# Gaps in the SBUF pools, so that the operands of the long products begin at multiples of 128 bytes

## The chip, the cores and the metric

The kernel runs on one core of a Trainium2 chip. The core has a matrix engine (TensorE; PE in the rows, and PEld for its weight loads), a vector engine (VectorE, DVE), a scalar engine (ScalarE, ACT), GpSimd (POOL), SyncE (SP), which issues most transfers, and 16 DMA engines between HBM and the on-chip memories. SBUF holds operands in 128 partitions; a tile lies at the same byte address in each. PSUM takes the products. The metric is the time of one execution on the device, in microseconds.

## The reference

Two transformer blocks on 256 tokens of 2048 features, all in float32.

```python
# first block
h = h + mixer_sublayer(rms_norm(h, norm_mix[l]), w_in[l], ..., w_out[l])
h = h + peer_sublayer(rms_norm(h, norm_ffn[l]), peer_w_query[l], peer_sub_keys[l], peer_u[l], peer_v[l])
# peer_sublayer, of each block of 128 tokens
q = (hb @ w_query).reshape(PEER_BLOCK, PEER_HEADS, 2, D_KEY // 2)
...
a = jax.nn.gelu(jnp.einsum('thkd,td->thk', u_sel, hb), approximate=False)
return jnp.einsum('thk,thkd->td', (g * a).astype(hb.dtype), v_sel)
```

The mixer runs two kinds of attention over 16 meta tokens and the 256 tokens. The product-key experts choose 16 of 16384 experts per head and token. The second block has a modulation vector, attention beside a diagonal state space, two gated branches, and a feed-forward of 5632 hidden features with a causal convolution. Nearly all the arithmetic is in products of a weight [features in, features out] with the activations [features in, 256 tokens].

## The kernel before

**Products.** Activations lie with features on partitions, so a product takes 128 x 128 of a weight as the stationary operand and 128 features of all 256 tokens as the moving one (272 columns in the mixer, with the meta tokens). To keep float32's precision in the fast mode (float32r), each operand is split into a high and a low part, and `mm3` issues three products: high by high (L175), high by low (L176), low by high (L177). Each of the three loads its own weights; PE's records show a weight load (PEld) beside every product.

```python
mm(out, a[0], b[0], start=start, stop=False, **kw)
mm(out, a[0], b[1], start=False, stop=False, **kw)
mm(out, a[1], b[0], start=False, stop=stop, **kw)
```

**Stages**, in the order of time:
- the mixer (to some 500 us): its norm makes hh and hl with 272 columns, so 1088 bytes per row; heads go into tiles hd of the same size. The products of w_out read hd;
- the experts: queries, then scores of all experts against hh, hl of the next norm (1024 bytes per row), while routing runs; from about 950 to 2100 us the loop over expert rows does, per half step, 24 products with rows of v (stationary wp or, for odd rows, vp; moving ahi, alo) and 24 products of scores (stationary wp, moving hh, hl); a stretch of the former alone follows;
- attention and state space (2290 to 2750 us), with hh, hl of another norm and the pool's tiles b2 (named b in the trace); then the branches and the output product, whose moving operand is b2;
- the feed-forward (from about 3010 us): up products with hh, hl, down products with act, in four turns.

**Tiles.** A pool lays its tiles out in the order in which their names are first asked for, a ring of `bufs` copies for each, each address rounded to 32 bytes. The pool `glob` lives throughout and holds raw (a ring of 5 loads), constants, the residual xT, hh, hl, wp (a ring of 8 split weights) and the norm's scratch. Other pools are opened per stage behind it and hold hd, ahi, alo, vp, first, b2 and act.

```python
hi, lo = (self.sb(self.glob, "wp", [128, n, m], F32R, bufs=NWP) for _ in range(2))
...
hi, lo = (sb(spare["v"], "vp", [128, 1024], F32R, bufs=2) for _ in range(2))
...
hi, lo = (sb(spare["v"], nm, [128, T], F32R, bufs=10) for nm in ("ahi", "alo"))
...
A[j + f] = a = sb(pool, "act", [128, 2, T], F32R, bufs=26)
```

**Order.** The program's order is written out by hand: `Pipe` issues the loads and splits of a job between the products of the job one or two places before, and side work (attention heads, routing, state space, `ssm_parameters`) advances by a step behind each job. Weights come by SyncE's queue into raw, are split by ScalarE (L143) and VectorE (L144), and are multiplied. `ssm_parameters` (L1683) loads three small tables at the end of the experts' loop: raw takes two of them, the tiles ldt and sel2 of the pool `experts` stand beside it.

Of the kernel before, what the change touches and what calls it, by code (L numbers as in the profile page):

```python
# [8 lines left out]
F32 = mybir.dt.float32  # L9
# [15 lines left out]
EPS = 1e-6  # L25
# [11 lines left out]
class Pipe:  # L37
    """Issues jobs in order. A job is its preparation and its matmuls, each a function that may be a generator of steps;
    the preparation is issued between the steps of the matmuls of the job `depth` places before.
    Side work (generators) advances by one step behind each job, and behind those steps of it that `mid` names;  # L40
    so does `slow`, which nothing here completes."""
# [8 lines left out]
    @staticmethod  # L50
    def steps(f, *args):
        """f as a generator that returns f's result."""
        r = f(*args)
        if hasattr(r, "send"):
            r = yield from r
        return r
# [58 lines left out]
class Core:  # L115
# [13 lines left out]

    def ps(self, tag):  # L130
        return self.psum.tile([128, 512], F32, name=f"ps_{tag}", tag=f"ps_{tag}", bufs={"g": 2, "t": 2, "v": 4}[tag])

    def copy(self, out, in_):
        """A copy, on the scalar and the vector engine in turn."""
        self.flip ^= 1
        if self.flip:
            self.nc.scalar.copy(out, in_)
        else:
            self.nc.vector.tensor_copy(out, in_)

# [8 lines left out]
    def parts(self, kt, m):  # L149
        """The two parts of kt * 128 rows of m: tiles of at most 1024 elements per partition. Returns the tiles  # L150
        [(first k, n, hi, lo)] and the function of k that gives its parts."""
        per = 1024 // m
        tiles = []
# [6 lines left out]
    def split_w(self, loaded, kt, off, m):  # L160
        """The parts of a loaded weight's columns off .. off + m."""
# [10 lines left out]
    def mm3(self, out, a, b, start, stop, **kw):  # L172
        """out += a.T @ b for operands in two parts each (the product of the low parts, under 2^-24, is left)."""
        mm = self.nc.tensor.matmul
        mm(out, a[0], b[0], start=start, stop=False, **kw)  # L175
        mm(out, a[0], b[1], start=False, stop=False, **kw)  # L176
        mm(out, a[1], b[0], start=False, stop=stop, **kw)  # L177

    def load_w(self, w, r0, kt, c0, width, pieces=1):
        """[kt * 128, width] of a weight, in tiles of at most 2048 elements per partition: [(first kt, n, tile)]."""  # L180
# [16 lines left out]
    def gemm_jobs(self, w, r0, kt, c0, ncols, xs, n, post, group=256):  # L197
        """out[f, :n] = w[r0:r0 + kt * 128, c0 + f].T @ x, in feature tiles of 128; post(f tile, psum) takes each.
        xs(k) gives the parts of x's k-th 128 rows."""
# [23 lines left out]
    def lead(self, w, r0, c0, xs, n, post, before):  # L223
        """The first four feature tiles of a gemm of 16 k tiles whose x is made meanwhile: by before(c) for k = 4 c .. 4 c + 3,
        in two steps.
        A generator: its first step takes only the pools that live throughout, and the last job before it is issued there."""
# [63 lines left out]
    def columns(self, pool, name, vecs, stage, queue=None):  # L290
        """Vectors of DRAM, each a multiple of 128 long, as columns [128, n], and the generator that fills them:
        a tile of each 128 rows is turned on the PE."""
# [3 lines left out]
        at = 0  # L296
# [24 lines left out]
    def rstd(self, out, ss, n):  # L321
        """out = 1 / sqrt(ss / n + EPS)"""
# [5 lines left out]
    def head_sum(self, acc, h, sq, n):  # L328
        """Adds the sums of sq's columns as the rows h and 32 + h of acc."""
        self.nc.tensor.matmul(acc[:40, :n], self.sel[:, 7 - h:47 - h], sq, start=h == 0, stop=h == 7)  # L330

    def head_parts(self, out, src):
        """The parts of rows that are the same on h and 32 + h."""
# [3 lines left out]
    def head_row(self, h, n=128):  # L337
        """What a product with head_parts' rows takes to give row h on n partitions."""
        return self.both[:, h:h + 1].to_broadcast([40, n])

# [1 line left out]
    def sq_add(self, k, t):  # L342
        """Adds the squares of the residual's k-th tile; they are issued at the next call."""
# [24 lines left out]
    def norm(self, gains, shifts=None, table=None):  # L368
        """The parts of the normalised residual, x * rstd * gain (+ shift): a function of k, and one that makes
        the parts of k = 4 c .. 4 c + 3 in two steps, to be called for c = 0, 1, 2, 3."""  # L370
# [59 lines left out]
    def stagger(self, gens, every):  # L430
        """Side work: starts a generator every so many steps; a step of each live one per step, the oldest first."""
# [14 lines left out]
    def interleave(self, gens, width):  # L446
        """Side work: runs the generators, `width` of them at a time, a step of each per step."""
# [13 lines left out]
    def mixer(self, pool, upto):  # L461
# [46 lines left out]
        def gains():  # L508
            """What is needed later only."""
# [13 lines left out]
        # the rows, turned to [feature, position], 16 meta and 256 tokens: the residual, and its parts times the gain  # L523
        self.xT = [sb(self.glob, "xT", [128, T], bufs=KT) for _ in range(KT)]
        hh = sb(self.glob, "hh", [128, KT, N], F32R)
# [37 lines left out]
        def scales():  # L563
            """1 / rms of each position, along the free axis; the products take it behind."""
# [6 lines left out]
        def scaled(out, p, o, factor=None):  # L571
            """The product, scaled."""
# [7 lines left out]
        xs_tok = lambda k: (hh[:, k, NM:], hl[:, k, NM:])  # L580
        hd = lambda dt=F32: sb(pool, "hd", [128, N], dt, bufs=40)
# [10 lines left out]
        def values(key):  # L592
            """Values to [position, head dim], the positions in tiles of 128, 128 and 16."""
# [17 lines left out]
        # the heads' outputs times their gains, in parts, and the sums of the outputs' squares  # L611
# [18 lines left out]
        def scale_of(key):  # L630
            """1 / rms of the heads' outputs, on every partition."""
# [52 lines left out]
        # forget gates: log f = min(z, 0) - log(1 + exp(-|z|)), summed along the positions  # L684
# [18 lines left out]
        # forgetting attention  # L703
# [167 lines left out]
    def slowly(self, chunks, every):  # L871
        """Side work: a step of the modulation's first chunks every so many steps."""
# [5 lines left out]
    def modulate(self, chunks):  # L878
        """Completes the first chunks of the modulation."""
# [4 lines left out]
    def peer_head(self):  # L884
        """The norm and the first queries."""
# [17 lines left out]
    def peer(self, ctx, pool, upto):  # L903
# [16 lines left out]
        def start_u(i):  # L920
            """Expert rows i * 128 .. to [feature, expert], in parts: the step that turns the g-th four feature tiles,
            and the function of k that gives the parts."""
# [17 lines left out]
        def spill():  # L940
            """The parts of x to DRAM, [q, c, b, a, token] of feature 512 q + 128 a + 32 b + c."""
# [6 lines left out]
        def reorder():  # L948
            """The parts of x from DRAM: partition 32 q + c of tile 4 b + a."""
# [11 lines left out]
        def blocks(i):  # L961
            """As start_u, but turned on the vector engine in blocks of 32 x 32: partition 32 q + c of the k-th tile is
            feature 512 q + 32 k + c. Returns the step that turns a half and the one that parts it."""
# [17 lines left out]
        def scores(i, g, at):  # L981
            """A quarter of the scores."""
# [36 lines left out]
        def weights(b, chunks=slice(0, 16)):  # L1019
            """The weights of WI expert rows, [second key, chunk, first key, token]."""  # L1020
# [6 lines left out]
        def start():  # L1027
# [3 lines left out]
            def first(c, wc):  # L1031
                """The first weights, of the last chunks from where they are made."""
# [9 lines left out]
        def coef(i):  # L1042
# [5 lines left out]
            if i < 2:  # L1048
                hi, lo = (sb(wp, "first", [128, T], F32R, bufs=4) for _ in range(2))
            else:  # L1050
# [5 lines left out]
        def ahead(n):  # L1056
            """The coefficients for the n-th half step."""
# [10 lines left out]
        with self.tc.tile_pool(name="experts", bufs=1) as ep:  # L1068
            banks = {}
            spare["v"] = ep  # L1070

            def v_main(*ns):
                """The n-th half steps, of one half. Its first four tiles gather the sums of all experts, the others those of a block.
                Returns what adds the complete ones to the residual."""
# [34 lines left out]
            def half_step(n, block=None, half=0, ticks=0):  # L1109
                """The n-th half step, with the operands of the next, the coefficients of the second next and half of a block."""  # L1110
# [54 lines left out]
    def route(self, rp, wd, start_u, scores, spill, blocks, start, v_split, ahead):  # L1165
        """Weights of the chosen experts, [16 tokens' chunk, second key, first key, token], to DRAM; scores meanwhile."""
# [11 lines left out]
        def score():  # L1178
            """The scores of the next 128 experts as a job."""
# [21 lines left out]
        with self.tc.tile_pool(name="pick", bufs=1) as pool:  # L1201
# [3 lines left out]
            def turn_keys(g, bank):  # L1205
                """A quarter of the keys, turned; returns what moves them out."""
# [19 lines left out]
            def pick(vals, idx, src, width):  # L1226
                """The 16 largest of src's rows with their places, the earlier of equals first."""
# [193 lines left out]
    def reduce_angle(self, pool, a, shape, tag):  # L1421
        """a - 2 pi * round(a / (2 pi)), in place; 2 pi in three parts, of which the first two times a count are exact."""
# [11 lines left out]
    def sin_cos(self, sin, cos, a, tmp):  # L1434
        """Of angles in [-pi, pi]: the cosine is the sine of pi / 2 - |a|."""
# [5 lines left out]
    def mixing_head(self):  # L1441
        """The norm and the first inputs of the state space."""
# [7 lines left out]
    def mixing(self, pool):  # L1450
# [8 lines left out]
        # rotary tables  # L1459
# [21 lines left out]
        # projections  # L1481
# [9 lines left out]
        ssq = sb(pool, "ssq2", [40, 2, T], F32R)  # L1491

# [123 lines left out]
        # branches: gate = (1 + tanh) / 2, the half in the merged parts  # L1616
# [463 lines left out]
```

## Time and profile before

| | us |
|---|---|
| three runs | 3784.16, 3787.84, 3791.34 |
| median | 3787.84 |
| span of the profiled execution, first to last instruction | 3782.9 |
| TensorE busy / weight loads busy | 3702.9 / 3612.2 |
| VectorE / ScalarE / GpSimd busy | 2834.4 / 1820.2 / 479.0 |

The page gives the profiled execution's span alone; what lies around it is the difference to the runs, about 5 us. Busy time of PE is the union of records that overlap: a product's record lasts about 0.28 us, and the next begins some 0.11 to 0.13 us after it did. So a busy share near 100% doesn't tell how fast the products follow each other. That is read from counts in a window or from the starts in the timeline. A window counts every record that touches it.

### The profile page before, as it was taken

How to read it: one execution, taken by the hardware profiler on the slowest of the kernel's cores; microseconds unless marked ns; L12 is line 12 of the kernel's file. 1: busy time of each engine (PE TensorE's matmuls, PEld its weight loads, DVE VectorE, ACT ScalarE, POOL GpSimd, SP SyncE). 2: the span in 40 equal slices, each digit the busy share in tenths (PEclk: the TensorE clock that was granted, in tenths of full speed). 3: DMA queues.
4: the chain of work that ended last, by engine and by line, in shares of the span. 5: the costliest groups of instructions: out<-in, count | busy, mean ns of one | idle time of the engine just before them, and what ended most of it. 6: DMA issues, size and time to landing. Idle time of an engine off the chain costs nothing.

```text
span 3782.9 us, 72640 instructions
## 1 busy us (share of the span) xinstructions
PE 3702.9 (98%) x30186; PEld 3612.2 (95%) x30186; DVE 2834.4 (75%) x4414; ACT 1820.2 (48%) x2740; POOL 479.0 (13%) x496
## 2 busy tenths in 40 slices
PE   9999999999999999999999999899999999999998
PEld 8989899999999999999999999888889999999998
DVE  5555678977788888888888779999887675656565
ACT  4443443369444444444444456665544454444443
POOL 0000012100000000000000015666420100000000
PEclk9999999999999999999999999999999999999999
DMA  6546555445988888888888766555477665555563
GB/s 204 168 137 197 178 169 170 155 168 208 275 239 241 244 243 241 242 244 244 241 242 245 250 208 200 168 169 168 154 228 231 196 223 182 194 168 193 179 199 124
DMA packets 491481, 768.99 MB, mean 203 GB/s; under 512 B 21050, under 2 KB 332501, under 8 KB 485248
## 3 DMA queue, kind: packets, MB, share of 16 engines
q1 hardware_dynamic: 476160, 712.11, 61.2%
q0 software_dynamic: 14960, 52.23, 4.9%
q8 instruction: 237, 3.88, 0.4%
q14 instruction: 92, 0.75, 0.1%
q10 hardware_dynamic: 32, 0.01, 0.0%
HBM read 734.92 MB, written 27.26 MB: 201 GB/s over the span
## 4 chain that ended last, share of the span: by engine, by line
PE 83%; DVE 7%; ACT 5%; issue 2%; DMA 2%; POOL 1%; DVEq 0%; POOLq 0%; ACTq 0%
PE ps_g L175 19%; PE ps_g L177 19%; PE ps_g L176 19%; PE ps_v L175 4%; PE ps_v L176 4%; PE ps_v L177 4%; PE ps_t L175 3%; PE ps_t L176 3%; PE ps_t L177 3%; DVE wp L144 3%; ACT wp L143 1%; PE ps_t L934 1%; ACT raw L1366 1%; DMA raw<-in_peer_u_dram 1%; ACT hot_i L1381 1%
## 5 line engine op out<-in xcount | busy, mean ns | idle before, releaser
L175 PE MATMUL ps_g<-hh,wp 128*128 128x256 f32 (+1 forms) x5648 | 1629.0, 288 | 0.3 <-ACT wp L143 0.3
L177 PE MATMUL ps_g<-hh,wp 128*128 128x256 f32 (+1 forms) x5648 | 1606.9, 285 | 10.5 <-DVE wp L144 10.4
L176 PE MATMUL ps_g<-hl,wp 128*128 128x256 f32 (+1 forms) x5648 | 1604.6, 284 | 2.8 <-DVE hl L1614 2.8
L144 DVE TENSOR_TENSOR wp<-raw,wp 128x1024 fp32r<-128x1024 f32 (+2 forms) x877 | 1054.8, 1223 | 70.3 <-ACT wp L143 69.7
L175 PEld LDWEIGHTS ps_g<-hh,wp 128*128 128x128 f32 x5648 | 1079.8, 191 | 24.5 <-issue 15.6
L177 PEld LDWEIGHTS ps_g<-hh,wp 128*128 128x128 f32 x5648 | 1080.0, 191 | 14.3 <-DVE wp L144 13.5
L176 PEld LDWEIGHTS ps_g<-hl,wp 128*128 128x128 f32 x5648 | 1080.2, 191 | 3.7 <-DVE hl L1614 3.1
L143 ACT ACTIVATE wp<-raw 128x1024 fp32r<-128x1024 f32 (+2 forms) x877 | 869.4, 1014 | 379.0 <-PE ps_g L176 203.8
L862 DVE SCALAR_TENSOR_TENSOR macc<-raw,cs,macc 128x512 f32<-128x512 f32 x360 | 283.3, 787 | 0.0
L971 DVE STREAM_TRANSPOSE raw<-raw 128x1024 f32<-128x1024 f32 x196 | 242.6, 1238 | 36.9 <-DMA raw<-in_peer_u_dram 36.8
L1015 DVE TENSOR_TENSOR wp<-raw,wp 128x1024 fp32r<-128x1024 f32 x155 | 186.2, 1204 | 33.9 <-ACT wp L1013 33.9
L1013 ACT ACTIVATE wp<-raw 128x1024 fp32r<-128x1024 f32 x155 | 163.0, 1055 | 80.3 <-PE ps_t L176 46.8
L175 PE MATMUL ps_g<-act,wp 128*128 128x256 f32 x704 | 198.2, 282 | 1.0 <-ACT act L143 1.0
L990 ACT ACTIVATE gl<-ps_g 128x256 f32<-128x256 f32 x128 | 48.9, 382 | 310.3 <-PE ps_g L177 310.2
L176 PE MATMUL ps_g<-act,wp 128*128 128x256 f32 x704 | 196.9, 280 | 0.4
L177 PE MATMUL ps_g<-act,wp 128*128 128x256 f32 x704 | 196.4, 279 | 0.0
L1015 DVE TENSOR_TENSOR vp<-raw,vp 128x1024 fp32r<-128x1024 f32 x101 | 123.0, 1218 | 94.5 <-ACT vp L1013 94.3
L1024 POOL DMA_DIRECT2D wb<-wd x32 | 36.7, 1147 | 1162.7 <-DVE gl L1047 1134.3
L1052 ACT ACTIVATE ahi<-gl 128x256 fp32r<-128x256 f32 x126 | 52.5, 417 | 256.9 <-DVE gl L1047 256.9
L1953 DVE SCALAR_TENSOR_TENSOR cv<-ps_g,cols_b,cv 128x255 f32<-128x255 f32 x84 | 40.6, 483 | 174.2 <-ACT cv L1952 174.2
L175 PE MATMUL ps_v<-ahi,wp 128*128 128x256 f32 x612 | 170.3, 278 | 0.0
L176 PE MATMUL ps_v<-alo,wp 128*128 128x256 f32 x612 | 169.6, 277 | 0.0
(560 smaller groups left out, 7225.9 us busy)
## 6 DMA issues: line engine op xcount, KB each, us to landing
raw<-in_peer_v_dram SPq DMA_DIRECT2D x128, 1024.0 KB, 8.2
raw<-in_w_in_dram SPq DMA_DIRECT2D x118, 1024.0 KB, 7.2
raw<-in_peer_u_dram SPq DMA_DIRECT2D x392, 256.0 KB, 5.5
raw<-in_w_mod_dram SPq DMA_DIRECT2D x96, 1024.0 KB, 5.3
raw<-in_w_up_dram SPq DMA_DIRECT2D x87, 1024.0 KB, 6.6
raw<-in_w_out_dram SPq DMA_DIRECT2D x32, 1024.0 KB, 5.7
raw<-in_w_down_dram SPq DMA_DIRECT2D x32, 1024.0 KB, 7.1
raw<-in_peer_u_dram SPq DMA_DIRECT2D x30, 1024.0 KB, 5.1
```

Of the source, the lines that this page charges most:

```text
L143: self.nc.scalar.activation(hi, src, AF.Copy)
L144: self.nc.vector.tensor_tensor(lo, src, hi.bitcast(F32), op=OP.subtract)
L175: mm(out, a[0], b[0], start=start, stop=False, **kw)
L176: mm(out, a[0], b[1], start=False, stop=False, **kw)
L177: mm(out, a[1], b[0], start=False, stop=stop, **kw)
L862: nc.vector.scalar_tensor_tensor(acc, t[:, k], s, acc, op0=OP.mult, op1=OP.add)
L971: nc.vector.transpose(out=x, in_=x)
L990: nc.scalar.activation(a, p[:, :T], AF.Gelu)
L1013: nc.scalar.activation(hi, src, AF.Copy)
L1015: return lambda: nc.vector.tensor_tensor(lo, src, hi.bitcast(F32), op=OP.subtract)
L1052: nc.scalar.activation(hi, a, AF.Copy)
L1953: nc.vector.scalar_tensor_tensor(t[:, 1:], p[:, :T - 1], w[1], t[:, 1:], op0=OP.mult, op1=OP.add)
```

## The change

`gap` asks a pool for a tile that nothing writes or reads, so that what the pool lays out behind it begins later. Six gaps are placed: 96 bytes ahead of hh in `glob` (which shifts hh, hl, wp and all that follows), 32 ahead of hd, 96 behind the four tiles first, 64 ahead of vp, 96 ahead of b2, 64 ahead of act. To make room, ldt and sel2 lose their own tiles and become parts of the ring tile raw, which is asked for with 512 elements on 128 partitions instead of 256 on 32. No instruction is added, and every engine's order is the same; three instructions (the load of ldt, the copy to sel2 and the small product of L1706) have another address.

Where the operands of the products by three begin, in bytes modulo 128 of the program's addresses, and how many products of the program there are:

| moving, stationary | columns | before | after | products |
|---|---|---|---|---|
| hh or hl, wp | 256 | 32, 32 | 0, 0 | 15552 |
| ahi, alo or first, wp | 256 | 96, 32 | 0, 0 | 3720 |
| ahi, alo or first, vp | 256 | 96, 96 | 0, 0 | 2424 |
| act, wp | 256 | 96, 32 | 0, 0 | 2112 |
| b2, wp | 256 | 64, 32 | 0, 0 | 960 |
| mixer's hh or hl, wp | 272 | 32 and 96 in turn, 32 | 0 and 64 in turn, 0 | 1584 |
| mixer's hh or hl without the meta tokens, odd rows, wp | 256 | 96, 32 | 64, 0 | 576 |
| hd, wp | 256 | 0 and 64 in turn, 32 | 0 and 64 in turn, 0 | 768 |

(The even rows of the mixer's hh and hl are in the first line; 48 of the 1584 have weights of 8 columns, at every multiple of 32.) Weight slices are 512 bytes apart, moving slices 1024, except for the mixer's, so the place is the same for all slices of a tile. Tiles that are no operand of these products shift too: xT stays at 32, raw at 0.

```diff
+    def gap(self, pool, name, size):
+        pool.tile([128, size // 4], F32, name="gap_" + name, tag="gap_" + name, bufs=1)
...
         self.xT = [sb(self.glob, "xT", [128, T], bufs=KT) for _ in range(KT)]
+        self.gap(self.glob, "hh", 96)
         hh = sb(self.glob, "hh", [128, KT, N], F32R)
...
+        self.gap(pool, "hd", 32)
         hd = lambda dt=F32: sb(pool, "hd", [128, N], dt, bufs=40)
...
                 hi, lo = (sb(wp, "first", [128, T], F32R, bufs=4) for _ in range(2))
+                if i == 1:
+                    self.gap(wp, "first", 96)
...
             spare["v"] = ep
+            self.gap(ep, "vp", 64)
...
         ssq = sb(pool, "ssq2", [40, 2, T], F32R)
+        self.gap(pool, "b2", 96)
...
-        raw = self.raw_tile([32, 2, 128])
+        t = self.raw_tile([128, 512])
+        raw, ldt, sel2 = t[:32, :256].rearrange("p (a b) -> p a b", a=2), t[:2, 256:256 + NT], t[:2, 384:512].rearrange("p (a b) -> p a b", a=2)
...
-        ldt = sb(pool, "ldt", [2, NT])
...
-        sel2 = sb(pool, "sel2", [2, 2, 64])
...
         NB = 44
+        self.gap(pool, "act", 64)
```

## Rows read from the trace of the kernel before

**Rows 1.** The page, busy time of each engine, share of span, instructions.
```profile
PE 3702.9 (98%) x30186; PEld 3612.2 (95%) x30186; DVE 2834.4 (75%) x4414; ACT 1820.2 (48%) x2740; POOL 479.0 (13%) x496
```

**Rows 2.** The page, the chain that ended last, by engine and by line.
```profile
PE 83%; DVE 7%; ACT 5%; issue 2%; DMA 2%; POOL 1%; DVEq 0%; POOLq 0%; ACTq 0%
PE ps_g L175 19%; PE ps_g L177 19%; PE ps_g L176 19%; PE ps_v L175 4%; PE ps_v L176 4%; PE ps_v L177 4%; PE ps_t L175 3%; PE ps_t L176 3%; PE ps_t L177 3%; DVE wp L144 3%; ACT wp L143 1%; PE ps_t L934 1%; ACT raw L1366 1%; DMA raw<-in_peer_u_dram 1%; ACT hot_i L1381 1%
```

**Rows 3.** PE's waits: who waited for whom, us in total, times, longest.
```profile
PE ps_v L1874 <- POOL b L1861: 14.8, 14, 1.3
PE ps_g L177 <- DVE wp L144: 12.4, 15, 2.0
```

**Rows 4.** Windows that hold products of one kind alone, PE.
```profile
core 0: us, PE busy (x), PEclk, DMA share, GB/s
3260.00:3300.00 40.00, 40.00 (x336) 1.00 0.62 201
2940.00:2990.00 50.00, 50.00 (x426) 1.00 0.68 213
3160.00:3190.00 30.00, 30.00 (x257) 1.00 0.54 177
3555.00:3585.00 30.00, 30.00 (x267) 1.00 0.61 197
2160.00:2200.00 40.00, 40.00 (x356) 1.00 0.81 267
85.00:115.00 30.00, 30.00 (x240) 1.00 0.54 165
```

**Rows 5.** Timeline of PE, expert stage: start us, us, instruction; every 24th product.
```profile
1501.42 0.28 PE L175 MATMUL ps_v<-ahi,vp 128*128 128x256 f32 x1
...
1504.27 0.28 PE L175 MATMUL ps_g<-hh,wp 128*128 128x256 f32 x1
...
1507.14 0.29 PE L175 MATMUL ps_v<-ahi,wp 128*128 128x256 f32 x1
...
1509.88 0.28 PE L175 MATMUL ps_g<-hh,wp 128*128 128x256 f32 x1
```

**Rows 6.** Groups by line and tile: xcount | busy us, mean ns | idle before.
```profile
L175 PE MATMUL ps_g<-hh,wp 128*128 128x256 f32 (+1 forms) x5648 | 1629.0, 288 | 0.3 <-ACT wp L143 0.3
L175 PE MATMUL ps_g<-act,wp 128*128 128x256 f32 x704 | 198.2, 282 | 1.0 <-ACT act L143 1.0
L175 PE MATMUL ps_t<-ahi,wp 128*128 128x256 f32 x612 | 168.9, 276 | 0.0
L175 PE MATMUL ps_t<-ahi,vp 128*128 128x256 f32 x396 | 112.1, 283 | 0.0
```

**Rows 7.** Timeline of one-column products (L866), two cuts of one run.
```profile
367.96 0.73 PE L866 MATMUL ps_t<-ones,macc 128*128 128x1 f32 x6
...
367.96 0.95 PE L866 MATMUL ps_t<-ones,macc 128*128 128x1 f32 x8
```

**Rows 8.** Windows by stage, all engines.
```profile
core 0: us, PE busy (x) PEld busy (x) DVE busy (x) ACT busy (x) POOL busy (x), PEclk, DMA share, GB/s
950.00:2100.00 1150.00, 1143.21 (x9672) 1141.09 (x9671) 926.32 (x1111) 479.15 (x603) 33.76 (x33) 1.00 0.88 246
2290.00:2750.00 460.00, 426.32 (x3120) 393.04 (x3119) 422.01 (x546) 277.44 (x428) 269.87 (x238) 0.97 0.54 174
3150.00:3500.00 350.00, 349.79 (x2934) 349.21 (x2933) 206.41 (x283) 161.45 (x213) 0.00 (x0) 1.00 0.57 185
```

**Rows 9.** A group of PE in the window 2290 to 2750 us.
```profile
L175 PE MATMUL ps_g<-hh,wp 128*128 128x256 f32 x873 | 259.8, 298 | 0.0
```

**Rows 10.** The instructions on ldt: ns min/median/max, first and last start.
```profile
L1706 PE MATMUL ps_g<-ldt,sel x2: 271/271/271, 2127.1 to 2127.2; 2*128 2x32 f32 x2
L1697 POOL DMA_DIRECT2D ldt<-in_ssm_log_dt_dram x1: 710/710/710, 2107.9 to 2107.9; - x1
```

## The prediction

> **What bounds the kernel now.** I read the busy line of the page first [rows 1]: TensorE (PE) is busy for 3702.9 of 3782.9 us, its weight loads (PEld) for 3612.2, nothing else for more than 75%. The chain of work that ended last says the same: 83% of it is PE [rows 2]. Then PE's waits: the longest sums are 14.8 and 12.4 us [rows 3], so there is almost no waiting to remove. What can still be shortened is the time from the start of one product to the start of the next, and that has to be read from the trace, because a product's own duration (276 to 288 ns) overlaps its neighbours.
>
> I get this step in two ways. A window that holds products of one kind alone gives a count; a product lasts 0.28 us and is counted if it touches the window, so the step is (window + 0.28) / count. With [rows 4]: products that read the norm's output (hh, hl against wp) 40.28/336 = 119.9 ns; the state-space stage's b2 tiles against wp 50.28/426 = 118.0; act against wp 30.28/257 = 117.8 in one stretch and 30.28/267 = 113.4 in a later one; ahi, alo against wp 40.28/356 = 113.1; the mixer's 272 columns 30.29/240 = 126.2. The granted clock is 1.00 in all of them, the 2.4 GHz level, so 256 columns at one per cycle are 106.7 ns and no row reaches that. In the expert stage the kinds stand side by side [rows 5], 24 products between two rows: ahi, alo against vp 2.85/24 = 118.8; hh, hl against wp 2.87/24 = 119.6; ahi, alo against wp 2.74/24 = 114.2. The groups by tile agree: the same product lasts 283 ns with vp as its weights and 276 with wp [rows 6].
>
> That pair is the key. The same moving tile, the same PSUM tiles and the same engines around it give 119 or 114 ns, and the tiles differ only in where they lie. By the table of the change, moving and stationary tile lie at 96 and 96 (mod 128) in the slow case, at 96 and 32 in the fast one; hh and wp at 32 and 32 are slow; b2 and wp at 64 and 32 between. So the place matters, and the steps differ by whole portions: 120.0 - 113.3 = 6.7 ns is a sixteenth of 106.7, the time of 64 of the 1024 bytes. I read 113.3 as 17 portions of 64 bytes and 120 as 18.
>
> **The change part by part.** The gaps issue nothing and move nothing: every engine keeps its instructions in their order. They only shift addresses. After it all classes of the table stand at 0 and 0, apart from the mixer's own tiles, whose odd rows stand at 64 (1088 bytes apart). No row of the trace has a full-speed product with both operands at a multiple of 64, let alone 128, so its step is bounded by the nearest rows. Below: weight loads alone, with products of one column, follow each other at (0.95 - 0.73)/2 = 0.11 us [rows 7], so 112 ns is the floor. Above: 126.2, the slowest step read here. I take 113.3, the fast row, for this reason: a moving slice that begins at 32 or 96 touches 17 portions of 64 bytes, one that begins at 0 touches 16, and a weight slice 9 against 8. If 120 is 17 portions and one lost to a meeting with the weight load, 0 and 0 needs 16 and one lost, which is 17, or 113.3. The weak point is b2, which already begins at 64 and still steps 118.0; its weights lie at 32, though, and I put the difference down to them.
>
> The sum by classes, with the number of products from the table:
> hh, hl against wp, 15552 x (119.6 - 113.3 = 6.3) = 98.0 us. ahi, alo against vp, 2424 x 5.5 = 13.3 us. ahi, alo against wp, 3720 x about 0.5 (113.1 to 114.2 now) = 1.9 us. act, 2112 x 2.3 (half at 117.8, half at 113.4) = 4.9 us. b2, 960 x 4.7 = 4.5 us. Together 122.6 us. The mixer's remaining products (1584 of 272 columns, 576 of 256, 768 of hd) keep one operand at 64 every other time; between no gain and the full 6.3 I take half, 2928 x 3.1 = 9.1 us.
>
> From this goes what the stages can't take. From 950 to 2100 us PE is busy for 1143.2 of 1150 and DMA for 0.88 [rows 8]; a twenty-fifth less time raises that to about 0.92, which I let stand. From 2290 to 2750 us VectorE is busy for 422.0 of 460 and PE waits already, so of the 3 x 873 hh products there [rows 9], worth 16.5 us, I count half: 8.3 us off. Elsewhere (3150 to 3500 us) PE has 349.8 of 350 and the others have room, so the gain lands in full. Sum: 122.6 + 9.1 - 8.3 = 123 us.
>
> The other edit puts ldt and sel2 into the ring tile of raw. The same DMA (issued at 2107.9 us) and the same small product (2127.1 us) [rows 10] now hold that one ring slot, which the two transposes just ahead of the product held before; it comes free later by one product, 0.3 us. SyncE's next load into the slot waits that much longer, with four other slots filled: I cost it at 0, at 0.3 if the cover were gone.
>
> The sum is made against the profiled span, 3782.9; the three runs have their median 5 us above it (3787.84), which is start and end. 3787.84 - 123 = 3665 us.
>
> A rule speaks against the whole idea. The trace shows the step changing with the weights' place, 118.8 against 114.2 [rows 5]. The Trainium skill, page "SBUF — State Buffer", section "Who interferes with whom", says that PE has one read port for the moving operand and another, independent, for the weights, and that PE waits on nobody; by it the places could not matter and the sum would be 0. The trace does not agree with that for these products. The same skill's page "TensorE: Matmul & The Clock Gate", section "Back-to-back issue gap", gives N / 2.4 + 2.5 ns, 109.2 for 256 columns; no row here shows it, and by it the sum for hh alone would be 15552 x 10.4 = 162 us.
>
> **The rivals.**
> (a) Equal places collide. What is common to the slow rows is that both operands lie at the same place modulo 128 (32 and 32, 96 and 96), and the fast one has them 64 apart; 32 apart (b2) is between. If only the difference counts, 0 and 0 is the slow case again, for all classes: hh stays at 119.6, and ahi, alo against wp lose (119.6 - 113.9) x 3720 = 21.2 us, act 3.8 x 2112 = 8.0, b2 1.6 x 960 = 1.5, vp 0.8 x 2424 = 1.9. That is 33 us slower, 3821 us. For it: two slow pairs of equal place, smooth order by difference. Against: both begin in the middle of a 64-byte portion, so the trace can't tell equal from crooked. It decides from a step of 118.3 for 0 and 0 upward, the mean of the five classes' steps now by their counts; there the gain on hh no longer pays for the loss on ahi.
> (b) Half a cure. Aligned tiles step as b2 does now, 117.8: hh gains 1.8 x 15552 = 28 us, vp 2.4, ahi against wp loses 3.9 x 3720 = 14.5, act 4.2: about 12 us faster, 3776.
> (c) The place isn't the cause. vp and wp differ in something that the gaps leave alone (vp's ring of two is filled by other lines), and every step stays: 3788. Against it: hh and wp, filled by the same lines as act and wp, step 119.9 and 113.4. The rule of independent ports (the skill's SBUF page, above) would give the same time.
> (d) More than hoped: the step falls to the weight loads' 112: 1.3 x 24768 = 32 us more, 3633.
> (e) Worse than any: a second lost portion, 126: 6.4 x 24768 = 159 us, 3947.
>
> **How the numbers follow.** 113.3 has 0.40, (d) 0.06, (b) 0.10, (a) 0.32, (c) 0.08, (e) 0.04. The likeliest is 3665, its own range 3645 to 3690 (step 112.5 to 114.5, mixer and VectorE at either end). Cases of both signs hold most of the chance, so the range for 8 in 10 runs from that to (a): 3640 to 3825. Faster by over 0.2% (7.6 us, about what a measurement of this kernel can tell from no change): 0.40 + 0.06 + most of (b) = 0.54. Slower: (a) and (e) = 0.36. Within: (c) and the rest of (b) = 0.10.
>
> **What would show it.** In the profile after, 40 us of pure hh products should hold about 355 instead of 336, the vp groups should last 276 ns instead of 283 and the wp groups of ahi should stay at 276. If the hh stretch still holds 336 and the ahi groups rise to 283, (a) is right. If PE's waits grow between 950 and 2100 us, the gain was given back to DMA or VectorE there. Two readings would break the argument at its root: a vp group and a wp group that still differ although both lie at 0, or an hh stretch that changes while its groups' places did not.

## The result, and the profile after

| | us |
|---|---|
| before, median of 4 runs beside the change | 3788.32 (3784.16 to 3791.34) |
| after, median of 4 runs | 3818.31 (3818.25 to 3819.56) |
| ratio after / before | 1.0082, 95% interval 1.0068 to 1.0096 |
| span of the profiled execution, before / after | 3782.9 / 3817.8 |

The change costs 30 us. The forecast was 3665, a gain of 123; what came is rival (a), 3821. The page of after has the same numbers of instructions on every engine; PE and its weight loads are busy for 39 us more, the other engines within 2.4 us of before (columns as in [rows 1]):

```profile
PE 3742.0 (98%) x30186; PEld 3651.1 (96%) x30186; DVE 2836.6 (74%) x4414; ACT 1817.8 (48%) x2740; POOL 478.5 (13%) x496
```

Windows of after with one kind alone, as [rows 4]: hh, b2, act early and late, ahi against wp, the mixer's 272 columns:

```profile
core 0: us, PE busy (x), PEclk, DMA share, GB/s
3300.00:3340.00 40.00, 40.00 (x336) 1.00 0.62 201
2960.00:3010.00 50.00, 50.00 (x424) 1.00 0.66 212
3200.00:3230.00 30.00, 30.00 (x252) 1.00 0.65 208
3590.00:3620.00 30.00, 30.00 (x252) 1.00 0.58 188
2180.00:2220.00 40.00, 40.00 (x335) 1.00 0.78 262
85.00:115.00 30.00, 30.00 (x240) 1.00 0.56 173
```

The hh stretch holds 336 products, as before: 40.28/336 = 119.9 ns. The fast ones became slow: ahi against wp 40.28/335 = 120.2 (113.1 before), act 30.28/252 = 120.2 in both places (117.8 and 113.4), b2 50.28/424 = 118.6 (118.0). The mixer's 240 are as before. The clock is 1.00 in all. In the expert stage the kinds no longer differ. Four starts in after, 24 products apart, as [rows 5]:

```profile
1520.33 0.28 PE L179 MATMUL ps_v<-ahi,vp 128*128 128x256 f32 x1
...
1523.21 0.28 PE L179 MATMUL ps_g<-hh,wp 128*128 128x256 f32 x1
...
1526.09 0.28 PE L179 MATMUL ps_v<-ahi,wp 128*128 128x256 f32 x1
...
1528.97 0.28 PE L179 MATMUL ps_g<-hh,wp 128*128 128x256 f32 x1
```

Each takes 2.88/24 = 120.0 ns: hh, vp and wp alike. The groups say so too; against [rows 6], wp went from 276 to 283 and vp stayed:

```profile
L179 PE MATMUL ps_t<-ahi,wp 128*128 128x256 f32 x612 | 173.2, 283 | 0.0
L179 PE MATMUL ps_t<-ahi,vp 128*128 128x256 f32 x396 | 112.1, 283 | 0.0
```

PE's longest waits did not grow (14.8 and 12.4 in [rows 3]):

```profile
PE ps_v L1883 <- POOL b L1870: 13.3, 12, 1.3
PE ps_g L181 <- DVE wp L148: 11.7, 15, 2.0
```

So the time went into the step. A third of the time from the start of one `mm3` to the start of the next, from the two traces in order, with the operands' addresses from the programs, gives the mean step of each class:

| moving, stationary | before, ns | after, ns | products | difference, us |
|---|---|---|---|---|
| hh, hl / wp, 256 columns | 119.62 | 119.84 | 15552 | +3.4 |
| ahi, alo, first / wp | 113.88 | 119.99 | 3720 | +22.7 |
| ahi, alo, first / vp | 118.95 | 119.99 | 2424 | +2.5 |
| act / wp | 116.04 | 119.93 | 2112 | +8.2 |
| b2 / wp | 117.63 | 118.70 | 960 | +1.0 |

The sum is +37.8; the two spans differ by 34.9. b2 alone stays below 120: the table of the change has it at 0 and 0 modulo 128, but modulo 256 the program puts b2 at 0 and its weights at 128, a difference that experiment 1 reads at 118.7. The start of one and the same product, from trace to trace, moves by 18.1 us between 950 and 2100 us of before and by 8.6 from there to 2290, where ahi stands, and by 7.4 from 3010 to the end, where act stands.

### The profile page after: what moved, and what is told of

Same layout as the page of the kernel before. It is cut to its first block, busy times and chain, and to the rows that moved or that the text cites. A ratio compares the mean times of both kernels' runs of the same rounds, so it can differ in the third digit from the quotient of the medians.

```text
span 3817.8 us, 72639 instructions
## 1 busy us (share of the span) xinstructions
PE 3742.0 (98%) x30186; PEld 3651.1 (96%) x30186; DVE 2836.6 (74%) x4414; ACT 1817.8 (48%) x2740; POOL 478.5 (13%) x496
## 4 chain that ended last, share of the span: by engine, by line
PE 82%; DVE 8%; ACT 6%; issue 2%; DMA 2%; POOL 0%; DVEq 0%; POOLq 0%; ACTq 0%
PE ps_g L179 19%; PE ps_g L181 19%; PE ps_g L180 19%; PE ps_v L180 4%; PE ps_v L181 4%; PE ps_v L179 4%; DVE wp L148 3%; PE ps_t L181 3%; PE ps_t L180 3%; PE ps_t L179 3%; ACT wp L147 1%; ACT raw L1375 1%; PE ps_t L940 1%; DMA raw<-in_peer_u_dram 1%; ACT hot_i L1390 1%
## 5 line engine op out<-in xcount | busy, mean ns | idle before, releaser
L1021 DVE TENSOR_TENSOR vp<-raw,vp 128x1024 fp32r<-128x1024 f32 x101 | 123.1, 1218 | 113.4 <-ACT vp L1019 113.4
L179 PE MATMUL ps_g<-act,wp 128*128 128x256 f32 x704 | 200.7, 285 | 0.8 <-ACT act L147 0.8
L180 PE MATMUL ps_g<-act,wp 128*128 128x256 f32 x704 | 199.6, 284 | 0.3
L181 PE MATMUL ps_g<-act,wp 128*128 128x256 f32 x704 | 199.3, 283 | 0.0
L181 PE MATMUL ps_v<-ahi,wp 128*128 128x256 f32 x612 | 173.5, 284 | 0.0
L179 PE MATMUL ps_v<-ahi,wp 128*128 128x256 f32 x612 | 173.5, 284 | 0.0
L181 PE MATMUL ps_t<-ahi,wp 128*128 128x256 f32 x612 | 173.3, 283 | 0.0
```

Of the source, the lines that this page charges most:

```text
L1021: return lambda: nc.vector.tensor_tensor(lo, src, hi.bitcast(F32), op=OP.subtract)
```

## The experiments

Theory A: the difference of the two operands' places decides the step. Theory B: the place of each does, as the prediction took it. All ratios are to the kernel before, with 95% intervals. "Difference" is moving minus stationary in bytes.

**1. Products alone.** The kernel's loop, with nothing beside it:

```
for j in range(kts):
    k, q = j % 16, j % 8
    a = [W[:, s // 4 + i * 1024 + q * 128:][:, :128] for i in range(2)]
    b = [X[:, m // 4 + i * 4096 + k * 256:][:, :256] for i in range(2)]
    c.mm3(p, a, b, j == 0, j == kts - 1)
```

> This kernel leaves the whole of the two blocks out. It only issues products by three as mm3 does (128 x 128 weights, 256 columns), 96 in a row for each pair of places of the moving and the stationary slices: the moving ones begin at 0, 32, ... 480 and the stationary ones at 0, 32, 64 and 256 bytes modulo 512, all 64 pairs in order and once more in another order, with no other engine at work. Theory A (the difference decides): the step depends on moving minus stationary modulo 128 alone: 119.5 to 120 ns at a difference of 0, 113.3 at 64, about 117.7 at 32 and 96, and (0,0), (32,32), (64,64) read the same. Theory B (the absolute place decides, what the prediction took): moving slices at 0 and 64 are faster by 3 to 7 ns than those at 32 and 96, whatever the weights' place. Theory C (a longer period, 256 or 512 bytes): the fast pairs come back only every 256 or 512 bytes, so moving 64 against stationary 0 and moving 192 against 0 differ. If all steps are within 1 ns of each other here, the place alone doesn't set it and the other engines' traffic in the kernel takes part.

First product of nine blocks one behind the other, 96 products apart; the stationary slices at 0, the moving ones at 0, 32, ... 224, then 256 (start us, us, instruction):

```profile
88.61 0.28 PE L179 MATMUL ps_v<-X,W 128*128 128x256 f32 x1
...
100.12 0.28 PE L179 MATMUL ps_v<-X,W 128*128 128x256 f32 x1
...
111.44 0.28 PE L179 MATMUL ps_v<-X,W 128*128 128x256 f32 x1
...
122.75 0.28 PE L179 MATMUL ps_v<-X,W 128*128 128x256 f32 x1
...
134.25 0.28 PE L179 MATMUL ps_v<-X,W 128*128 128x256 f32 x1
...
145.65 0.28 PE L179 MATMUL ps_v<-X,W 128*128 128x256 f32 x1
...
156.91 0.28 PE L179 MATMUL ps_v<-X,W 128*128 128x256 f32 x1
...
167.82 0.28 PE L179 MATMUL ps_v<-X,W 128*128 128x256 f32 x1
...
179.18 0.28 PE L179 MATMUL ps_v<-X,W 128*128 128x256 f32 x1
```

The gaps over 96 are 119.9, 117.9, 117.8, 119.8, 118.8, 117.3, 113.6, 118.3 ns. Without the first products of each block (6 to 90), over all 64 pairs and both orders:

| difference modulo 256 | 0 | 32 | 64 | 96 | 128 | 160 | 192 | 224 |
|---|---|---|---|---|---|---|---|---|
| step, ns | 120.0 | 117.8 or 116.7 | 117.8 (one block of 16: 113.3) | 120.0 | 118.7 (one: 120.0) | 117.4 or 118.7 | 113.3 (four of 16: 117.8) | 118.4 |

(0, 0), (32, 32), (64, 64) and (256, 256) all read 119.9 to 120.0, so B falls. The difference decides, with no other engine at work, but it repeats every 256 bytes, not 128: 64 ahead and 64 behind are not the same. And at five of the eight differences, 192 and 64 among them, one pair of places can have two steps. That is theory C's period with A's difference; I call it A256 from here.

**2. One difference for all, and its mirror image.** Edits to the changed kernel for -64 (192 modulo 256); the mirror takes 192, 64, 32, 128 bytes for the four gaps:

```diff
+        self.gap(self.glob, "wp", 64)
...
+                if i == 2:
+                    self.gap(spare["v"], "ahi", 192)
...
-        self.gap(pool, "b2", 96)
+        self.gap(pool, "b2", 160)
...
-        self.gap(pool, "act", 64)
```

> The changed kernel, but the weights (wp and vp) lie 64 bytes further on than the moving slices for all the long products: moving at 128, weights at 192 modulo 256, for hh, hl, ahi, alo, act and b2 alike. That is moving minus stationary = -64. Theory A256 (the difference modulo 256 decides, with the steps of e1_map: 113.3, or 117.8 where a run is caught in the slower of two states): if most products stand at 113.9, which ahi against wp had in the kernel before at this difference, 24768 products gain 6 ns on the 120.0 they have after the change, 149 us, less 8 that the state-space stage can't take: 3677 us; if all were caught at 117.8 it would be 3764. Theory A128 (the difference modulo 128): the same, 3677. Theory B (both at multiples of 64, place by itself decides): no different from the changed kernel, 3818.

> The mirror image of e2_minus64: the weights lie 64 bytes ahead of the moving slices (moving at 128, weights at 64 modulo 256), moving minus stationary = +64. Theory A128: 64 apart is 64 apart, the same as e2_minus64, about 3677. Theory A256: the step of e1_map at a difference of 64, 117.8 in 15 of 16 blocks, so 24768 products gain 2.2 ns on 120.0, 54 us: 3764. Theory B: 3818.

Minus 64: 3725.33 median of 4, at 3699.02, 3703.46, 3747.20 and 3751.14; ratio 0.9862 (0.9792 to 0.9932). Plus 64: 3780.23, ratio 0.9981 (0.9971 to 0.9991). In the profiled execution of minus 64, one of the faster two, hh stands at 114.2 ns, ahi at 113.6 and 113.5, act 115.2, b2 113.4; plus 64 has every class within 0.2 ns of 117.8. Windows of plus 64, the same kinds as above (hh, ahi, b2):

```profile
3260.00:3300.00 40.00, 40.00 (x342) 1.00 0.61 199
2160.00:2200.00 40.00, 40.00 (x342) 1.00 0.78 263
2950.00:2990.00 40.00, 40.00 (x342) 1.00 0.62 191
```

40.28/342 = 117.8 in all, the step that A256 expected; of its 54 us the time kept 38. A128 and B are out. For minus 64 two numbers were off. By its steps, minus 64 is worth 142 us against the changed kernel and its profiled execution gains 3817.8 - 3701.7 = 116; of the other 26 us 15 are idle time of PE (span less busy: 75.8 after the change, 90.7 here), and 11 stay unexplained. And the times fall into two groups, which no theory had.

**3. Everything moved alike, and ahi and act put back.** The first keeps only the gap ahead of hh, so places change and differences don't (but for 96 products of first); the second adds only a gap of 192 ahead of ahi and drops that ahead of act.

> The changed kernel with the gap ahead of hh alone: hh, hl, wp, hd, ahi, alo, vp, b2 and act all lie 96 bytes later than in the kernel before, so their places modulo 128 change (hh and wp both at 128 modulo 256, a multiple of 128, as the change wants it) and every difference stays as it was before. Theories A: the time of the kernel before, 3788 within 0.2 per cent, hh against wp at 119.6 to 119.8, ahi against wp at 113.9, vp at 119, b2 at 117.6. Theory B: the step of hh against wp, which are now aligned, changes from before; by the prediction's 113.3 it would give 98 us, 3690.

> The changed kernel with ahi, alo and act alone moved 64 bytes ahead of their weights (64 against 128 modulo 256); hh, hl, b2 and wp, vp stay where the change puts them. Theories A: ahi against wp falls from 120.0 to 113.9 (3720 x 6.1 = 23 us), against vp from 120.0 to 113.9 too (2424 x 6.1 = 15), act to 116 (2112 x 3.9 = 8), hh stays at 120.0: 3818 - 46 = 3772. If the loss of the change came from something else than these differences (the mixer, VectorE's or ScalarE's tiles at other places), the time stays near 3818. Theory B: all at multiples of 64, so 3818.

3786.35, ratio 1.0006 (0.9996 to 1.0015), and 3773.76, ratio 0.9976 (0.9966 to 0.9986). Windows of hh and of ahi against wp, the first two of the kernel shifted alike, the other two of that with ahi and act put back:

```profile
3260.00:3300.00 40.00, 40.00 (x335) 1.00 0.59 194
2160.00:2200.00 40.00, 40.00 (x355) 1.00 0.79 270
```

```profile
3260.00:3300.00 40.00, 40.00 (x336) 1.00 0.62 200
2160.00:2200.00 40.00, 40.00 (x355) 1.00 0.76 262
```

hh now lies at a multiple of 128 beside a wp at a multiple of 128, and steps 120 as it did at 32 and 32. With hh left there, moving ahi, alo and act alone takes back the whole loss and vp's part of the forecast's gain: 3818 to 3774, where 3772 was expected.

**4. What picks the rhythm.** Blocks of 72 at each multiple of 8, entered in six ways (`PLAN` of differences and entries; the loop is that of experiment 1).

> Again only products by three, none of the two blocks, with no other engine at work: 72 at each difference moving minus stationary of 0, 8, ... 248 bytes, each entered in six ways: behind 24 products at a difference of 0, 64 or 96, or behind 24 at 0 and one product of 24, 88 or 152 columns. e2_minus64 came in two groups of times (3699 to 3703 and 3747 to 3751), and its profile holds stretches of 113.3 and of 117.7 at one and the same difference. Theory S (what ran just before picks one of two rhythms, which then hold): at 192 and at 64 the same pair of places gives 113.3 behind some entries and 117.8 behind others, at 0 always 120.0; the slow rhythm lasts to the end of the block. Theory O (other engines' traffic in the full kernel makes the slow rhythm): here, with no traffic, 192 gives 113.3 behind every entry. Between the multiples of 32, a smooth rule would give steps between their neighbours' (120.0 at 0, 117.8 at 32); a rule of whole portions would give plateaus. A difference that gives 113.3 behind all six entries would be the one to build the kernel on.

Product 18 and product 66 of four blocks, 48 apart: differences 112, 120 and 192 behind a block at 0, then 192 behind a block at 64.

```profile
322.20 0.28 PE L179 MATMUL ps_v<-X,W 128*128 128x256 f32 x1
...
327.64 0.28 PE L179 MATMUL ps_v<-X,W 128*128 128x256 f32 x1
...
333.35 0.28 PE L179 MATMUL ps_v<-X,W 128*128 128x256 f32 x1
...
339.13 0.28 PE L179 MATMUL ps_v<-X,W 128*128 128x256 f32 x1
...
436.64 0.28 PE L179 MATMUL ps_v<-X,W 128*128 128x256 f32 x1
...
442.08 0.28 PE L179 MATMUL ps_v<-X,W 128*128 128x256 f32 x1
...
800.85 0.28 PE L179 MATMUL ps_v<-X,W 128*128 128x256 f32 x1
...
806.50 0.28 PE L179 MATMUL ps_v<-X,W 128*128 128x256 f32 x1
```

5.44/48 = 113.3, 5.78/48 = 120.4, 113.3, and 5.65/48 = 117.7. At 192 it is 113.3 behind four entries and 117.8 behind two; at 64, 113.3 behind one; at 0 always 120.0. Theory S holds, O falls: the rhythm is set by what ran just before, with no traffic. By bytes the rule is neither smooth nor one of wide portions (104: 120.0, 112: 113.3, 120: 120.4 to 122.2). 112 alone gave 113.3 behind all six. Two steps at one difference are no matter of 64 and 192 alone: 8 gives 117.6 or 120.0 and 80 gives 118.3 or 120.0, by the entry.

**5. The kernel on 112, and 8 bytes further.** Experiment 2's edits with other sizes, and the later norms' hh and hl laid 16 bytes into their tiles (24 in the second kernel, `SHIFT = 6`):

```diff
+SHIFT = 4
...
+    def late_by(self, pool, name, n):
+        t = self.sb(pool, name, [128, n * T + SHIFT], F32R)
+        return t[:, SHIFT:SHIFT + n * T].rearrange("p (k t) -> p k t", k=n)
...
-        hh = self.sb(self.glob, "hh", [128, KT, T], F32R)
+        hh = self.late_by(self.glob, "hh", KT)
```

> The kernel built on e6_entry's one difference that gave 113.3 behind all six entries: hh and hl of the later norms (14976 of the 24768 products) begin 16 bytes into their tiles, 112 bytes behind their weights modulo 256 (144 against 32); ahi, alo, act and b2 stand 64 ahead of their weights (224 against 32, difference 192), as in e2_minus64. Nothing else differs from the changed kernel. Theory A256 with the two rhythms of theory S: hh holds 113.3 everywhere, so the time no longer falls into two groups by hh; from the changed kernel's 3818, hh gives 14976 x 6.5 = 97 us, ahi, alo and first 6144 x 6.5 = 40, act 2112 x 2.2 to 6.5 = 5 to 14, b2 5. Of such sums e2_minus64's best runs kept 115 of 143; with the same share 3698, in full 3665. If it is caught in the slow rhythm all the same, over 3720. Rival: tiles that begin at 16 modulo 32 cost ScalarE and VectorE time when they write them; then PE's waits grow and it is no faster than e2_minus64.

> e7_112 with the norm's hh and hl 8 bytes further on (152 against 32, a difference of 120 instead of 112), and nothing else. Theory A256: e6_entry reads 120.4 at 120 and 113.3 at 112, so the 14976 hh products lose 7.1 ns each, 106 us, or some 85 with the share that waits take back: about 3790. If the difference counts in portions of 32 or 64 bytes, 8 bytes change nothing and the time is that of e7_112.

3721.07, ratio 0.9828 (0.9815 to 0.9842), all five runs within 3717.55 to 3723.72; and 3788.63, ratio 1.0008 (0.9998 to 1.0017). Eight bytes cost 67.6 us where 85 to 106 were expected: hh steps 121.5 on average against 115.0, 97 us by the steps. Of the 29 us that did not reach the time, PE's idle time accounts for 24: it is 72.2 us here and 96.7 in the kernel on 112. The feed-forward's hh windows, of the kernel on 112 and of that on 120:

```profile
3215.00:3255.00 40.00, 40.00 (x355) 1.00 0.64 210
```

```profile
3270.00:3300.00 30.00, 30.00 (x248) 1.00 0.60 196
```

40.28/355 = 113.5 and 30.28/248 = 122.1. The one group of times came as expected; 3698 did not. Over the whole kernel hh stands at 115.0, not 113.4, and 14976 x 1.6 = 24 us is the miss: in the feed-forward it is at 113.3, but in the experts' loop, by triples between 1000 and 2000 us, only half of them. PE's waits are not what differs from minus 64: the longest sum is 17.2 us in both.

**6. Groups of 24 in turn.** Products alone, 24 at one difference and 24 at another.

> Products alone again, with no other engine at work. As in the experts' loop, 24 products at one difference and 24 at another take turns, five times each; the first (where ahi stands, 0, 32, ... 224) against the second (where hh could stand, 0, 16, ... 240). e7_112 came to 3721, not 3698: its hh products stand at 113.3 in the long runs of the feed-forward, but in the loop, where each 24 follow 24 of ahi at 192, half of them are at 117.7. Theory S (the rhythm carries over from one group to the next): the pair 192 and 112 repeats that here, ahi near 113.5 and hh near 115.2 on average, without any traffic; 192 and 192 gives 113.3 in both; 0 and 0 gives 120.0; 192 and 0, as in the kernel before, about 113.9 and 119.6. Rival: the slow products of the loop come from its traffic (transfers at 0.91 of their time, writes of ScalarE and VectorE); then hh at 112 gives 113.3 here behind 192.

Starts in the pair 192 and 112: a group at 192, the next one, at 112, that one's thirteenth product, and the group behind it.

```profile
3016.26 0.28 PE L179 MATMUL ps_v<-X,W 128*128 128x256 f32 x1
...
3018.99 0.29 PE L179 MATMUL ps_v<-X,W 128*128 128x256 f32 x1
...
3020.42 0.28 PE L179 MATMUL ps_v<-X,W 128*128 128x256 f32 x1
...
3021.78 0.28 PE L179 MATMUL ps_v<-X,W 128*128 128x256 f32 x1
```

2.73/24 = 113.8 for the 24 at 192, then 2.79/24 = 116.3 for the 24 at 112 (means of the turns: 113.6 and 116.4). 192 and 192 gives 113.3 on both sides, 192 and 0 gives 114.1 and 119.2, 0 and 0 gives 120.0. So the loop's half-slow hh comes without traffic, and the rival falls. But theory S's reason, a rhythm carried over from the group before, does not fit the starts inside the group at 112: its first twelve products take 1.43/12 = 119.2 ns, its last twelve 1.36/12 = 113.3. The slow rhythm of the group before is not there to be carried over (113.8), and the fast one comes within the group. In the loop of the kernel on 112 each group of hh does the same: the first four `mm3` step between 116 and 128 ns on average, the last four 113.4. What a change from one difference to the other costs here is a passage of some twelve products; where both groups have the same difference there is none.

**7. Both together, and the second group of times.** Minus 64 everywhere, but the feed-forward's norm lays hh and hl 176 bytes into their tiles (difference 112):

```diff
-        self.xs, make = self.norm(a2, mod[:, 48:64], table="silu_and_others")
+        self.xs, make = self.norm(a2, mod[:, 48:64], table="silu_and_others", late=LATE)
```

> The choice that e9_pairs reads as best: 64 ahead of the weights (difference 192) for all long products, as in e2_minus64, but the feed-forward's hh and hl at 112 (4224 products in long runs). In e9_pairs 192 with 192 holds 113.3 on both sides and 192 with 112 reads 113.6 and 116.4, so the experts' loop stays at 192. Theory S: the feed-forward's hh is at 113.3 in every execution, whatever happened before it; the loop is at 113.3 when it is entered in the fast rhythm and at 117.8 when not, 9700 products x 4.4 = 43 us, so the executions still fall into two groups, at about 3695 and 3735. If the two groups of e2_minus64 came from the feed-forward alone, there is one group here, below 3705.

> e2_minus64 once more, for a profile of its other group of times. Theory S: where this execution is near 3750, its trace holds 40 us and more of difference in long stretches of 117.7 at places where e2_minus64's profile had 113.3, above all in the experts' loop, with the clock, the waits and the transfers alike; where it is near 3700, it has none there. If the slower group came from waits or transfers, the steps would be the same and the idle time larger.

The mixed kernel: 3706.62 median of 6 (3701.07 to 3732.05), ratio 0.9807 (0.9785 to 0.9829), the best median of this study, though its interval overlaps that of the kernel on 112; by the two ratios it is 2.7% below the change. Minus 64 again came to 3718.75, between its two groups, so there are not two fixed times. Windows of the first execution of minus 64 and then of the second: two in the experts' loop, one in the feed-forward.

```profile
1560.00:1600.00 40.00, 40.00 (x356) 1.00 0.95 254
1660.00:1700.00 40.00, 40.00 (x355) 1.00 1.00 268
3540.00:3570.00 30.00, 30.00 (x257) 1.00 0.56 181
```

```profile
1560.00:1600.00 40.00, 40.00 (x342) 1.00 0.89 244
1660.00:1700.00 40.00, 40.00 (x342) 1.00 1.01 269
3540.00:3570.00 30.00, 30.00 (x267) 1.00 0.62 208
```

The same program at the same addresses: 113.2 and 113.5 or 117.8 ns in the loop, and the other way about in the feed-forward, 117.8 or 113.4. The second execution ran the loop at 113.3 until 1441 us and then at 117.8 up to some 2100. The place where it turned, PE's timeline and VectorE's write of the low part of vp:

```profile
1440.41 1.18 DVE L1022 TENSOR_TENSOR vp<-raw,vp 128x1024 fp32r<-128x1024 f32 x1
...
1441.41 0.28 PE L179 MATMUL ps_v<-ahi,vp 128*128 128x256 f32 x1
1441.53 0.28 PE L180 MATMUL ps_v<-alo,vp 128*128 128x256 f32 x1
1441.64 0.38 PE L181 MATMUL ps_v<-ahi,vp 128*128 128x256 f32 x1
1441.87 0.28 PE L179 MATMUL ps_v<-ahi,vp 128*128 128x256 f32 x1
```

One product, the first that reads the low part of a new vp, is a tenth of a microsecond late; some 5500 products behind it step 117.8. I take it for a wait on that low part: the profile names no releaser, but VectorE's write ends at 1440.41 + 1.18 = 1441.59 us, just before. The first execution has such a place too: a product that starts at 1164.00 us takes as long (0.38 us), and the step goes from 113.5 to 118.0 until the one-column products at 1194 us, behind which 113.5 comes back. Yet the same one-column products pass seven times between 1441 and 2010 us of the second execution and the slow rhythm stays, and in the mixed kernel's trace the product that was late at 1164 starts 0.9 us late and the step stays at 113.5. So a late product stood ahead of both turns, but what decides whether a disturbance turns the rhythm is not shown. In the mixed kernel's profile the feed-forward's hh is at 113.39 and the loop at 113.3; its one run at 3732 would fit a loop that was at 117.8 for most of its time, but that execution has no trace, so this is argued.

## Why the prediction was wrong

**What bounds the kernel, and that the place matters:** right. PE's step is the time, the engines' order and waits stayed, and moving nothing but addresses takes this kernel from 3699 to 3818.

**The step that failed** is the value for 0 and 0: "If 120 is 17 portions and one lost to a meeting with the weight load, 0 and 0 needs 16 and one lost, which is 17, or 113.3". It measured 120.0 [rows 4 against the windows of after]. Counting portions that a slice touches has no part in it: hh at 128 beside wp at 128 steps as at 32 and 32 (experiment 3), and 64 pairs of places order by their difference, but for the two rhythms (experiment 1). The text itself named the weak point, b2, which began at 64 and stepped 118.0, and put it down to the weights' crooked place. It was the counterexample; so was act, which [rows 4] show at 117.8 and at 113.4 with one pair of places. I averaged the two; they are the two rhythms at a difference of 192.

**The sum by classes** then has the wrong sign: -122.6 forecast, +37.8 by the steps. The product counts were right, and rival (a)'s terms nearly: 21.2, 8.0, 1.5 and 1.9 against 22.7, 8.2, 1.0 and 2.5, with 3.4 for hh that it had at nothing. Its 3821 is 2.7 us from what came. Its reason was right in kind and wrong in detail: it took the difference modulo 128, so 64 apart as fast in either direction. Only the direction that the trace before showed, ahi 64 ahead of wp, is; the other gives 117.8 (experiment 2).

**The mixer's 9.1** did not come: 126.8 and 125.4 ns for its rows before, 126.8 and 125.4 after. Its rows are 1088 bytes apart and walk through four differences modulo 256, by the programs 0, 64, 128 and 192 both before and after.

**What the stages take.** Minus 64 shows it, since it has nearly the steps that the forecast wanted: against before they are worth 104 us (142 less 37.8) of its 122.6. The loop took almost its whole share: from 950 to 2100 us the same product comes 40.2 us earlier, of 44 by the forecast's terms, with the transfers at 0.93 of their time where 0.92 was estimated; the feed-forward gave 24.4. From 2290 to 2750 us it gained 1.7 of the 16.5 us of [rows 9]; the forecast let half stand there. The two spans differ by 81.2, so 23 of the 104 us did not reach the time, where the forecast took off 8.3. So even nearly the hoped-for step did not bring 3665: the best run of any kernel here is 3699.

**ldt and sel2** cost nothing to be seen: their product starts at 2145.9 us against 2127.1 in [rows 10], 18.8 later, of which 17.4 had come by 2100 us; and the kernel of experiment 3 that has this edit with all differences kept is at 1.0006.

**Range and chances.** 3818 is inside 3640 to 3825, but the forecast's sign had 0.54 against 0.36 for slower. Against (a) stood only that both slow pairs were also crooked. That the order by difference was already smooth over five classes, and that the forecast's own rule needed an excuse for one of them, should have put (a) first.

**The rule that the trace spoke against.** Experiment 1 moves the step between 113.3 and 120.0 ns by the operands' places with PE alone at work. The Trainium skill, page "SBUF — State Buffer", section "Who interferes with whom", gives PE two independent read ports and lets only the port pair of VectorE and GpSimd contend; by it all blocks would step alike. The runs do not agree with that. The prediction's other figure from the Trainium skill, 109.2 ns (page "TensorE: Matmul & The Clock Gate", section "Back-to-back issue gap"), is stated there for isolated products, not for a stream that loads weights for each; measured by starts, no class of products by three steps below 113.3 in any run, so the 162 us worked out from it had no ground here.

## What to carry to other kernels

Where each product loads its own weights, read the step by pairs of tiles, and set the places of the two operands against each other, not to a round address: here only a few offsets at odd multiples of 8 were slower than equal places, and alignment brought every class of the sum but b2 to the 120 ns of equal places. Measure the map of differences first, with the kernel's own pattern and nothing beside it; one such run gave what the argument from portions had wrong. Build on a pair that is fast behind every entry (112 in long runs), or that all its neighbours share (192 throughout the loop): a change of difference cost some twelve products in experiment 6.

## What the hardware showed that I had not expected

The step of these products depends on moving minus stationary modulo 256 bytes and falls on exact values that return (113.3, 116.7, 117.8, 118.7, 120.0). Measured by starts, no class of products by three went below 113.3, with weight loads alone at 112 [rows 7]. At differences of 64 and 192 there are two rhythms, 113.3 and 117.8, and other differences have pairs of their own (32: 116.7 and 117.8). What ran before sets which one comes; a single product late by 0.1 us was followed by 0.66 ms of the slower one, though not every late product does that. So one program at one set of addresses takes from 3699 to 3751 us, at the same granted clock (0.99 in all four runs). In the products alone all slices of an operand lie at multiples of 256 bytes from one another, so those runs can't tell whether a moving slice meets its own weights or those loaded beside it for the next product; why the two streams meet in this way no run shows either.
